# Out-projection by seven products for all eight token tiles, and norm one's scale and offset moved behind the transposes

## The chip, the cores and the metric

The kernel runs on one NeuronCore of a Trainium2 chip. The metric is the device time of one execution in microseconds. Four compute engines matter: PE (TensorE, matrix products), DVE (VectorE), ACT (ScalarE) and POOL (GpSimd). SP issues most of the transfers; in the changed kernel POOL issues some too. Each engine executes its own queue in order, and the queues meet at semaphores.

## The reference

One layer of a post-norm encoder on 1024 tokens of 1024 features, in float32. What matters here is the second half:

```python
mix = (gate_a * y_a + gate_b * y_b) @ w_out[l]
x = layer_norm(DEEPNORM_ALPHA * x + mix, ln1_g[l], ln1_b[l])
gu = x @ w_ffn_in[l]
g, u = jnp.split(gu, 2, axis=-1)
ffn = (jax.nn.silu(g) * u) @ w_ffn_out[l]
x = layer_norm(DEEPNORM_ALPHA * x + ffn, ln2_g[l], ln2_b[l])
```

`y_a` is a windowed attention, `y_b` a stick-breaking attention, and `layer_norm` takes mean and variance over the 1024 features of a token (epsilon 1e-5), then multiplies by a gain g and adds an offset b. `DEEPNORM_ALPHA` is 2 to the power 1/4; the kernel calls it ALPHA.

## The kernel before

**Precision.** Every matrix operand is split in two parts: `split` writes a rounded high part (a cast, on ACT) and the remainder (a subtraction, on DVE). A product is three matmuls: high times high, high times low, low times high. `mm3` issues them for a list of operand pairs, lines 116, 117 and 119. A matmul of 128 by 128 by 512 is written 128x512 below.

**Seven products.** A 2 by 2 block product can be formed with seven block products in place of eight, after sums of blocks on both sides (Strassen's scheme in Winograd's form). The FFN uses it for all tokens (`pair_steps`, matmuls on line 179, `run_pairs` sets the order), the down projection too (line 1512). The out-projection uses it for the first four token tiles only.

**Stages.** In-projections and gates, the two attentions with their branch projections, then: branch B's projection (`yBps`, loop over feature tiles c in the order 6, 7, 5, 4, 2, 3, 1, 0; n counts them), whose result is multiplied by the gate and added to branch A's, giving the transposed mix `mA`; `m_sums` forms its block sums as soon as two blocks exist, and `high` splits the others. Then the out-projection: for the token tiles tt 0 to 3 products p in the order 1, 2, 6, 5, 7, 3, 4 with two token tiles each (line 1369, weights' sums loaded and split by `begin_wo`, lines 550 and 551); after each, `take_in` adds the bank `ops` to the tile `acc` (x times ALPHA, line 1348). For tt 4 to 7 plain products by `mm3`, the two column halves one after the other. When a token tile has both halves, `norm_1` works on it (`layer_norm`, lines 1183 to 1191): statistics on DVE, the inverse root of the variance as a power on POOL (line 1187), then two 128x1024 operations on DVE that apply mean and g, and inverse root and b. The normed rows are stored to `x1_dr` for the residual and transposed on PE (line 1209, bank `x1ps`) by `x1_operands`, copied by ACT to `x1raw` (first four token tiles) or `x1low` (the others) and split to `x1A`.

**FFN.** `plain_half` does one column tile f = 0 by plain products, first on `x1A` of the first token half while the second half's norm ends, then on the second. Then 21 column tiles f by seven products in pairs; in each `left_f` and `right_f` load and split weights (`wlf`, `wrf`, `wbf`, `waf`, `wcf`), and `next_piece` makes one of the down projection's left operands (`left_sums`, tiles `sl`, stored to `s_dr`). Last the down products, norm two and the output.

**What sets the order.** A scheduler orders the instructions of each engine from the program's order and the dependencies; instructions marked `keep_in_program_order` stay as written. Tiles live in pools of slots by tag (`SLOTS`, 8 of tag `op`), and a new tile waits until the last reader of its slot is done. PSUM has eight banks in four tags (`BANKS`).

Of the kernel before, what the change touches and what calls it, by code (L numbers as in the profile page):

```python
# [48 lines left out]
def hybrid_trunk_kernel(ctx: ExitStack, tc, x, xt, w_first, w_v, w_in, b_gate, rel_bias, w_proj,  # L49
                        w_out, ln1_g, ln1_b, w_ffn_in, w_ffn_out, ln2_g, ln2_b, out):  # L50
# [747 lines left out]
    def value_steps(hd, g, wt):  # L798
# [9 lines left out]
        for i, kb in enumerate(kbs):  # L808
# [16 lines left out]
            def mult(i=i, kb=kb, lo_q=lo_q, n=n, pts=pts):  # L825
# [130 lines left out]
    def squash(t, c, br):  # L956
        col = br * 8 + c
        if c >= N_SQUASHED:
            tc.keep_in_program_order(
                nc.scalar.activation(t, t, AF.Sigmoid, bias=bg[:, col:col + 1]))  # L960
# [49 lines left out]

# [73 lines left out]
    m_high = [None] * 8  # L1084
    raw_22 = slot("pt", "m22")
    m_first = [slot(tag, f"m1_{kt}", F32R) for kt, tag in enumerate(("yt", "yt", "yt", "pt"))]
    m_ab = [[None] * 4 for _ in range(2)]
    acc_t = []

    def quarter(q):  # L1090
        return slice(q * 2 * P, (q + 1) * 2 * P)

    def m_sums(kt, a, b):

        put, sub = nc.vector.tensor_tensor, ALU.subtract
        g, (q0, q1, q2, q3) = m_first[kt], (quarter(q) for q in range(4))
        split(g[:, q2], g[:, q3], b[:, q0])
        nc.scalar.copy(raw_22[:, quarter(kt)], b[:, q1])
        put(b[:, q1], a[:, q1], b[:, q1], ALU.add)
        put(a[:, q1], a[:, q0], a[:, q1], sub)  # L1100
        put(a[:, q0], b[:, q1], a[:, q0], sub)
        put(b[:, q0], b[:, q0], a[:, q0], sub)
        for n, t in enumerate((a, b)):
            o = m_ab[n][kt] = slot("bw", f"m{'ab'[n]}_{kt}", F32R)
            split(o[:, LO], o[:, HI], t[:, LO])
# [533 lines left out]
```

## Time and profile before

| what | value |
|---|---|
| median of three runs | 1413.27 us (1411.41 to 1413.41) |
| profiled execution | 1412.51 us, its span 1410.7 us |
| granted TensorE clock, mean | 0.999 |
| PE busy | 1399.7 us, 99% of the span |
| DVE busy | 1034.1 us, 73% |
| ACT busy | 699.0 us, 50% |
| POOL busy | 236.0 us, 17% |
| seven products of the out-projection | 681.64 us, for 38.08 us, 168 matmuls |
| first matmul of the FFN's `plain_half` | at 766.72 us |

The span runs from the first instruction to the last. A busy share is the time in which an engine executes, over the span; PE overlaps successive matmuls, so each has a duration of 389 ns and starts about 227 ns after the one before it. In rows of a group, the columns are line, engine, operation, names written and read, shape and count, then the busy time, the mean of one in ns, and the idle time before it with what ended it. In rows of a timeline the first number is the start and the second the duration.

### The profile page before, as it was taken

The numbers are of one execution on the slowest core, as the hardware profiler recorded it, in microseconds if no ns is written. First come the engines' busy times: TensorE is split into PE (matmuls) and PEld (weight loads), VectorE is DVE, ScalarE is ACT, GpSimd is POOL, SyncE is SP. The second block draws the span as 40 slices with busy tenths as digits, with TensorE's granted clock in tenths as the row PEclk, the third lists the DMA queues.
The fourth block names the chain that finished last, engine by engine and source line by source line (L and its number), as shares of the span: only waits on it lengthen the run. The fifth ranks groups of instructions, "written<-read, shape, count | busy, mean of one in ns | idle before, by whom it ended". The sixth has DMA issues, their size and how long they took to land.

```text
span 1410.7 us, 18935 instructions
## 1 busy us (share of the span) xinstructions
PE 1399.7 (99%) x6642; PEld 1164.6 (83%) x6642; DVE 1034.1 (73%) x1671; ACT 699.0 (50%) x1245; POOL 236.0 (17%) x308
## 2 busy tenths in 40 slices
PE   9999999999999999999999999999999999999997
PEld 7888888888888888888888888888888888888886
DVE  8967657545887788878998967767677765847666
ACT  6544444545888888774413644434444443322220
POOL 0000000002555878750001000000000000000033
PEclk9999999999999999999999999999999999999999
DMA  7476468856676478755651144433444349996652
GB/s 254 165 286 224 178 236 303 295 179 238 212 231 208 130 252 281 253 198 194 231 202 75 61 148 166 149 141 143 164 164 149 143 144 342 411 385 236 233 194 90
DMA packets 98927, 292.28 MB, mean 207 GB/s; under 512 B 9728, under 2 KB 26112, under 8 KB 98832
## 3 DMA queue, kind: packets, MB, share of 16 engines
q1 hardware_dynamic: 98832, 291.07, 58.2%
q8 instruction: 52, 0.85, 0.3%
q14 instruction: 43, 0.35, 0.1%
HBM read 187.20 MB, written 100.17 MB: 204 GB/s over the span
## 4 chain that ended last, share of the span: by engine, by line
PE 94%; DVE 2%; DMA 1%; ACT 1%; issue 1%; POOL 0%; DVEq 0%; SPq 0%; ACTq 0%; POOLq 0%
PE sxf L179 16%; PE d L1512 15%; PE sxp L179 9%; PE szf L179 8%; PE v L481 5%; PE gps L606 4%; PE szp L179 4%; PE syf L179 4%; PE yAps L910 3%; PE ops L1369 3%; PE syp L179 2%; PE tp_b L817 2%; PE tp_a L817 2%; PE plain L347 1%; PE pv_b L833 1%; PE pv_b L832 1%
## 5 line engine op out<-in xcount | busy, mean ns | idle before, releaser
L1512 PE MATMUL d<-wd,sl 128*128 128x512 f32 (+1 forms) x924 | 207.7, 387 | 0.0
L1512 PEld LDWEIGHTS d<-wd,sl 128*128 128x128 f32 x924 | 172.3, 188 | 35.4
L1532 POOL TENSOR_TENSOR mv<-mv,neghalf 128x1 f32<-128x1 f32 x8 | 9.0, 1121 | 606.7 <-DVE mv L1531 606.7
L109 ACT CAST wd<-wd 128x512 fp32r<-128x512 f32 x77 | 45.9, 621 | 114.1 <-PE d L1512 66.8
L794 POOL TENSOR_TENSOR w_b<-w_b,kp_b 128x511 f32<-128x511 f32 (+3 forms) x96 | 96.0, 1012 | 23.2 <-DVE kp_b L789 16.7
L110 DVE TENSOR_TENSOR sl<-h,sl 128x512 fp32r<-128x512 f32 x77 | 52.6, 686 | 27.6 <-ACT sl L109 27.6
L789 DVE TENSOR_TENSOR_SCAN kp_b<-kp_b,ident_ps 128x512 f32<-128x512 f32 (+2 forms) x64 | 56.5, 885 | 21.0 <-ACT kp_b L786 20.0
L109 ACT CAST sl<-h 128x512 fp32r<-128x512 f32 x77 | 47.5, 620 | 48.1 <-PE syf L179 18.3
L1489 DVE TENSOR_TENSOR x<-d,x 128x512 f32<-128x512 f32 (+1 forms) x41 | 27.6, 675 | 47.6 <-PE d L1512 47.5
L786 ACT ACTIVATE kp_b<-sc_b 128x512 f32<-128x512 f32 (+3 forms) x96 | 48.3, 504 | 28.0 <-PE sc_b L706 23.6
L110 DVE TENSOR_TENSOR wd<-wd,wd 128x512 fp32r<-128x512 f32 x77 | 52.7, 709 | 10.7 <-ACT wd L109 10.6
L179 PE MATMUL szf<-x1S63h,wcf 128*128 128x512 f32 x168 | 55.1, 389 | 0.0
L110 DVE TENSOR_TENSOR pt_b<-tp_b,pt_b 128x512 fp32r<-128x512 f32 (+1 forms) x96 | 49.9, 544 | 6.6 <-ACT pt_b L109 5.7
L729 POOL MEMSET bias<- 64x64 f32 x2 | 0.3, 145 | 314.3 <-ACT bias L725 314.3
L109 ACT CAST pt_b<-tp_b 128x512 fp32r<-128x512 f32 (+1 forms) x96 | 46.6, 503 | 8.0 <-PE tp_b L817 7.6
L759 POOL TENSOR_SCALAR w_a<-w_a,st_a 128x640 f32<-128x640 f32 (+2 forms) x64 | 42.2, 669 | 48.0 <-PE sc_a L706 26.6
L754 ACT ACTIVATE w_a<-w_a,st_a 128x640 f32<-128x640 f32 (+2 forms) x64 | 44.7, 700 | 8.6 <-DVE st_a L748 7.5
L787 ACT ACTIVATE w_b<-sc_b 128x511 f32<-128x511 f32 (+3 forms) x96 | 48.3, 504 | 0.0
L817 PE MATMUL tp_b<-ident,w_b 128*128 128x128 f32 x288 | 47.3, 272 | 0.2
L110 DVE TENSOR_TENSOR pt_a<-tp_a,pt_a 128x512 fp32r<-128x512 f32 (+1 forms) x96 | 44.6, 486 | 3.3 <-ACT pt_a L109 2.2
L1307 ACT ACTIVATE h<-sxf 128x512 f32<-128x512 f32 x21 | 12.6, 598 | 68.2 <-PE sxf L179 68.2
L817 PEld LDWEIGHTS tp_b<-ident,w_b 128*128 128x128 f32 x288 | 36.4, 140 | 11.1 <-DVE pt_b L110 1.1
(1574 smaller groups left out, 4285.2 us busy)
## 6 DMA issues: line engine op xcount, KB each, us to landing
s_dr<-sl SPq DMA_DIRECT2D x77, 512.0 KB, 2.6
sl<-s_dr SPq DMA_DIRECT2D x77, 512.0 KB, 7.6
wLf<-in_w_ffn_in_dram SPq DMA_DIRECT2D x22, 512.0 KB, 4.3
wRf<-in_w_ffn_in_dram SPq DMA_DIRECT2D x22, 512.0 KB, 3.6
wd<-in_w_ffn_out_dram SPq DMA_DIRECT2D x22, 512.0 KB, 8.2
v_dr<-vc SPq DMA_DIRECT2D x16, 512.0 KB, 3.4
qs<-q_dr SPq DMA_DIRECT2D x16, 512.0 KB, 6.7
kh<-k_dr SPq DMA_DIRECT2D x16, 512.0 KB, 6.5
```

The source lines that it names most:

```text
L109: return (nc.scalar.copy(dst_h, src), nc.vector.tensor_tensor(dst_l, src, dst_h.bitcast(F32), ALU.subtract))
L110: nc.vector.tensor_tensor(dst_l, src, dst_h.bitcast(F32), ALU.subtract))
L179: mm(acc, lw[:, ks], rx, start=(first and kt == i == 0), stop=(kt == 3 and i == 2), skip_group_check=not first)
L481: mm(accs[j], a, b, start=(first and kt == n == 0), stop=(kt == 3 and n == 2), skip_group_check=True)
L606: mm(acc[hf], lw[:, ks], rx[k][:, (LO, HI)[hf]], start=(k == j == 0), stop=(k == KT - 1 and j == 2))
L754: nc.scalar.activation(s[:, 0:w], s[:, 0:w], AF.Exp, bias=st[:, m:m + 1], scale=-1.0, accum_out=st[:, 2:3])
L786: nc.scalar.activation(kp[:, c0:e], sc[:, 0:n], AF.Sigmoid, scale=-1.0)
L787: nc.scalar.activation(be[:, m0:e], sc[:, m0 - c0:n], AF.Sigmoid)
L789: nc.vector.tensor_tensor_scan(kp[:, 0:e], kp[:, 0:e], ident_ps()[:, 0:e], 0.0, ALU.mult, ALU.add)
L794: nc.gpsimd.tensor_tensor(be[:, m0:e], be[:, m0:e], kp[:, m0 - 1:e - 1], ALU.mult)
L817: ins = tr(tp[:, (qb - lo_q) * P:(qb - lo_q + 1) * P], wt[qb - q0][:, (kb - qb) * P:(kb - qb + 1) * P], ident)
L1512: mm(part, a, b, start=(fresh and i == k == 0), stop=(i == n - 1 and k == 2), skip_group_check=not fresh)
```

## The change

- The out-projection goes by seven products for all eight token tiles (`project_out(p, j)`, four token tiles j per product, p in the order 1, 2, 5, 3, 6, 7, 4). Sums and splits of the mix and of the weights are set beside its tiles and beside branch B by a table `aside`.
- Everything in this stage is divided by ALPHA: products 1, 5 and 3 are scaled by ACT into `acc`, and POOL's queue adds the rows of x by an adding DMA (`plus`); products 2, 6, 7 and 4 are added by DVE.
- The orders of DVE, ACT and POOL's queue in this stage are written out as chains (`chain`, `chain_s`, `tied`): each instruction comes after the one before it in its lane.
- `norm_1` forms only (x - mean) times the inverse root: power and one multiply on POOL, one activation of 128x1024 on ACT. g and b are applied behind the transposes, where a feature is a partition: ACT's copy out of the bank has a scale and a bias (`scaled`, from a small tile `gb_1`).
- The rows stored in `x1_dr` have neither g nor b. During the FFN POOL loads half a row tile, loads g, multiplies, stores (`scale_x1`, two pieces for each of the eight token tiles, behind the eleven of `left_sums`), and adds b by an adding DMA.
- f = 1 of the FFN has its seven right operands split ahead of time (`split_f1`); the signs of some sums change; in the down stage ALPHA is applied with each addition (`take_down`).

```diff
-    for p in (1, 2, 6, 5, 7, 3, 4):
...
-        for j in range(2):
...
-            take_in(t0 + j, cs, accs[j], scale)
-            if p in (3, 4):
-                norm_1(t0 + j)
...
-    for hf, cs in enumerate((LO, HI)):
-        for tt in range(4, 8):
...
-            mm3(acc, pairs)
-            take_in(tt, cs, acc)
...
+    def project_out(p, j):
+        accs = by if p in (2, 5, 3) else bx
+        first = p in (1, 2, 5)
+        if first:
+            accs[j] = bank(("tr", "tr", "tr", "pv")[j] if accs is by
+                           else ("mm", "mm", "sc", "sc")[j], f"ops{p}_{j}")
+        for i, kt in enumerate(KT_ORDER):
...
+            for n, (a, b) in enumerate(((lh, wh), (lh, wl), (ll, wh))):
+                mm(accs[j], a, b, start=(first and i == n == 0), stop=(i == 3 and n == 2),
+                   skip_group_check=not first)
+        tt, cs = j + 4 * (p in (5, 7, 4)), (LO, HI)[p in (5, 7, 3, 6)]
...
+        if p in (1, 5, 3):
+            chain_s(nc.scalar.activation(t, accs[j], AF.Copy, scale=1 / ALPHA))
+            plus(t, x_rows(tt, cs))
+        else:
+            chain(nc.vector.scalar_tensor_tensor(t, accs[j], 1 / ALPHA, t, ALU.mult, ALU.add))
...
+    for p in OUT[:5]:
+        for j in range(4):
+            project_out(p, j)
+            for work in aside[p, j]:
+                work()
+            if p == 6:
+                norm_1(j)
+    for n, (p, j) in enumerate(((7, 0), (7, 1), (4, 0), (7, 2), (4, 1), (7, 3), (4, 2), (4, 3))):
+        project_out(p, j)
+        if n > 3:
+            x1_operands(0, acc_t, (n - 4,))
+        if p == 4:
+            norm_1(j + 4)
...
-        nc.vector.scalar_tensor_tensor(t, t, mv[:, 0:1], g, ALU.subtract, ALU.mult)
-        if quick:
-            for cs in cuts:
-                nc.vector.scalar_tensor_tensor(t[:, cs], t[:, cs], mv[:, 2:3], b[:, cs],
-                                               ALU.mult, ALU.add)
...
+    def norm_1(tt):
+        mv, t = statistics(f"1_{tt}", 2, chain), acc_t[tt]
+        nc.gpsimd.tensor_scalar(mv[:, 3:4], mv[:, 0:1], mv[:, 2:3], -1.0, ALU.mult, ALU.mult)
+        chain_s(nc.scalar.activation(t, t, AF.Identity, bias=mv[:, 3:4], scale=mv[:, 2:3]))
...
-                    nc.scalar.copy(part, tps[i])
-                    split(o[:, LO], o[:, HI], part)
+                    scaled(part, tps[i], kt + 4 * i)
+                    halve(o[:, LO], o[:, HI], part)
...
+    def scaled(dst, src, k):
+        chain_s(nc.scalar.activation(dst, src, AF.Identity, bias=gb_1[:, 8 + k:9 + k],
+                                     scale=gb_1[:, k:k + 1]))
...
+    aside = {
...
+        (2, 0): [part(sum_4, 2), part(wo_split, 3, 1)],
+        (2, 1): [part(sum_4, 3), part(wo_split, 3, 0)],
...
+        (6, 2): [part(wo_split, 4, 1)],
+        (6, 3): [part(wo_split, 4, 0)]}
...
+    def scale_x1(tt, cs):
+
+        t, queue = slot("op", f"x1g{tt}_{cs.start}"), nc.gpsimd
+        queue.dma_start(t[:, LO], x1_dr[tt][:, cs])
+        queue.dma_start(t[:, HI], rows_of(ln1_g, cs))
+        queue.tensor_tensor(t[:, LO], t[:, LO], t[:, HI], ALU.mult)
+        queue.dma_start(x1_dr[tt][:, cs], t[:, LO])
+        done = [tt - 1] * (cs == LO and tt > 0) + [7] * (cs == HI and tt == 7)
+        for k in done:
+            queue.dma_start(x1_dr[k], rows_of(ln1_b, slice(0, D)), accum_op=ALU.add)
```

In the excerpts a row is line, operation, tile written, tiles read and shape. `ops_0`, `ops_1`, `ops_2` are the banks of token tiles j = 0, 1, 2, `m` the split mix, `woh` and `wol` the weights' high parts and remainders, `acc` the rows of a token tile; the last number tells copies of a name apart.

On PE, before, the end of product 3 and the start of product 4 in the seven products (bank `ops_0_7289`):

```order
L1369 MATMUL ops_1_7414<-wh_o_1_7432,mb_7106 128x512
L1369 MATMUL ops_1_7414<-wh_o_1_7432,mb_7153 128x512
L1369 MATMUL ops_1_7414<-wl_o_1_7433,mb_7153 128x512
L1369 MATMUL ops_1_7414<-wh_o_1_7432,mb_7153 128x512
L1369 MATMUL ops_0_7289<-wh_ot_0_7472,m22h 128x512
L1369 MATMUL ops_0_7289<-wl_ot_0_7473,m22h 128x512
```

In the changed kernel, on PE, the end of (7, tile 1) and the start of product 4 on tile 0's bank:

```order
L1411 MATMUL ops_1_7250<-wol_0_7587,m_0_7603 128x512
L1411 MATMUL ops_1_7250<-woh_0_7586,m_0_7603 128x512
L1411 MATMUL ops_2_7273<-woh_1_7565,m_2_7594 128x512
L1411 MATMUL ops_2_7273<-wol_1_7566,m_2_7594 128x512
L1411 MATMUL ops_2_7273<-woh_1_7565,m_2_7594 128x512
L1411 MATMUL ops_2_7273<-woh_1_7565,m_3_7597 128x512
L1411 MATMUL ops_0_7219<-woh_1_7658,m_2_7093 128x512
L1411 MATMUL ops_0_7219<-wol_1_7659,m_2_7093 128x512
```

Before, three tiles of other banks lay between product 7's and product 4's work on one bank; now one tile and four matmuls do, and the rest of (7, tile 2) follows behind (4, tile 0).

On DVE, before, the end of the seven products (`ln1g` and `ln1b` are g and b on all partitions):

```order
L1348 SCALAR_TENSOR_TENSOR acc_7054<-acc_7054,ops_0_7400 128x512
L1183 BN_STATS bn_0_7493<-acc_7054 128x6
L1186 BN_AGGR mv_0_7494<-bn_0_7493 128x2
L1188 SCALAR_TENSOR_TENSOR acc_7054<-acc_7054,mv_0_7494,ln1g 128x1024
L1191 SCALAR_TENSOR_TENSOR acc_7054<-acc_7054,mv_0_7494,ln1b 128x1024
L1348 SCALAR_TENSOR_TENSOR acc_7056<-acc_7056,ops_1_7414 128x512
```

In the changed kernel, on DVE, product 6's tiles 2 and 3, up to the eviction of (7, tile 0):

```order
L1419 SCALAR_TENSOR_TENSOR acc_7165<-ops_2_7273,acc_7165 128x512
L1207 BN_STATS bn_2_7558<-acc_7165 128x6
L110 TENSOR_TENSOR wol_1_7659<-wor_1_7590,woh_1_7658 128x1024
L1215 BN_AGGR mv_2_7662<-bn_2_7558 128x2
L1419 SCALAR_TENSOR_TENSOR acc_7166<-ops_3_7296,acc_7166 128x512
L1207 BN_STATS bn_3_7583<-acc_7166 128x6
L110 TENSOR_TENSOR wol_0_7682<-wor_0_7592,woh_0_7681 128x1024
L1215 BN_AGGR mv_3_7685<-bn_3_7583 128x2
L1419 SCALAR_TENSOR_TENSOR acc_7399<-ops_0_7219,acc_7399 128x512
```

The two 128x1024 operations of a norm have left DVE; the remainders of product 4's weights stand ahead of the statistics' end, and the eviction that frees the bank stands behind both.

On ACT, before, the transposed tiles of the first token half:

```order
L1219 COPY x1raw_7791<-x1ps_1_7781 128x512
L1219 COPY x1raw_7791<-x1ps_5_7786 128x512
L109 CAST x1A_1_7792<-x1raw_7791 128x512
L109 CAST x1A_1_7796<-x1raw_7791 128x512
L1219 COPY x1raw_7810<-x1ps_2_7800 128x512
```

In the changed kernel, on ACT, the last of them with the norms of token tiles 6 and 7:

```order
L109 CAST x1A_2_7866<-x1raw_7861 128x512
L1397 ACTIVATE acc_7403<-acc_7403,mv_6_7870 128x1024
L1226 ACTIVATE x1raw_7899<-x1ps_3_7889,gb_7209 128x512
L109 CAST x1A_3_7900<-x1raw_7899 128x512
L1226 ACTIVATE x1raw_7899<-x1ps_7_7894,gb_7209 128x512
L109 CAST x1A_3_7904<-x1raw_7899 128x512
L1397 ACTIVATE acc_7405<-acc_7405,mv_7_7908 128x1024
L109 CAST wf_4_7914<-wLf_7213 128x512
```

The norms, which DVE carried, now stand in ACT's queue between the copies of the transposed tiles.

More of the change, by code (lines that the diff above doesn't have):

```diff
@@ L167, in product @@
     def product(acc, W, ops, p, first):
-        if p == 3:
+        if "all" in W:
+            wh, wl = (W["all"][p][:, cs] for cs in (LO, HI))
+        elif p == 3:
             wh, wl = W["c"][:, LO], W["c"][:, HI]
@@ L1081, in hybrid_trunk_kernel, with tied, chain, chain_s @@
     fill_until(1e9)
[L1084 to L1105, printed above, removed]
+    acc_t, m_raw = [], {}
+    m_ops = {p: [None] * 4 for p in range(1, 8)}
+    wo = {}
+    OUT = (1, 2, 5, 3, 6, 7, 4)
+    KT_ORDER = (2, 3, 1, 0)
+    put, sub = nc.vector.tensor_tensor, ALU.subtract
+    lanes = dict(s=last_y[:1], v=last_y[1:])
+    def tied(lane, ins):
+        for before in lanes.get(lane, ()):
+            tc.add_manual_dep(ins.ins, before.ins.name, mybir.DependencyInfo(
+                mybir.DependencyClass.NoSync, mybir.DependencyReason.DATA), reason="lane")
+        lanes[lane] = [ins]
+        return ins
+    def chain(ins):
+        return tied("v", ins)
+    def chain_s(ins):
+        return tied("s", ins)
+    def halve(dst_h, dst_l, src):
+        hi, lo = split(dst_h, dst_l, src)
+        chain_s(hi)
+        chain(lo)
+    def plus(dst, src):
+        tied("p", nc.gpsimd.dma_start(dst, src, accum_op=ALU.add))
+    def x_rows(tt, cs):
+        return x[tt * P:(tt + 1) * P, cs]
     def more_acc(tag):
@@ new lines, in sum_3, with sum_1, sum_2, sum_4 @@
+    def sum_3(kt):
+        a = m_raw[kt + 4]
+        chain(put(a[:, LO], a[:, HI], a[:, LO], sub))
+    def sum_1(kt):
+        a, b = m_raw[kt + 4], m_raw[kt]
+        chain(put(a[:, HI], a[:, HI], b[:, HI], ALU.add))
+    def sum_2(kt):
+        a, b = m_raw[kt + 4], m_raw[kt]
+        chain(put(b[:, HI], b[:, HI], a[:, LO], ALU.add))
+    def sum_4(kt):
+        b = m_raw[kt]
+        chain(put(b[:, LO], b[:, LO], b[:, HI], sub))
+        m_split(3, kt)
+    def part(f, *args):
+        return lambda: f(*args)
@@ L1228, in x1_operands @@
                     part = low[:, (LO, HI)[i]]
-                    nc.scalar.copy(part, tps[i])
+                    scaled(part, tps[i], kt + 4 * i)
                     split(o[:, LO], o[:, HI], part)
@@ new lines, in split_f0, with split_f1 @@
+    def split_f0(n):
+        key, t, tag = (("hl", L0, "op"), ("hr", R0, "bw"))[n]
+        h, l = Wf[0][key] = [slot(tag, f"wf0{key}{i}", F32R) for i in "hl"]
+        halve(h, l, t)
+    def split_f1(p):
+        src, terms, tag = {1: (x_, (), "op"), 5: (x_, (y_, x_), "bw"), 6: (x_, (u_, x_), "bw"),
+                           2: (z_, (), "op"), 4: (z_, (z_, x_), "bw"), 7: (y_, (y_, u_), "bw"),
+                           3: (u_, (), "bw")}[p]
+        if terms:
+            chain(put(src, *terms, sub))
+        o = Wf[1].setdefault("all", {})[p] = slot(tag, f"wf1_{p}", F32R)
+        halve(o[:, LO], o[:, HI], src)
@@ new lines, in hybrid_trunk_kernel @@
+    for p in OUT[:5]:
[11 more added lines that the diff above has]
+            norm_1(j + 4)
+        if n == 1:
+            split_f1(2)
+            for tt in range(4):
+                dma(x1_dr[tt], acc_t[tt])
@@ L1422, in hybrid_trunk_kernel @@
+    for p in (4, 7, 3):
+        split_f1(p)
+    with tc.issue_after(wo["last"].ins), tc.issue_after(lanes["v"][0].ins):
+        left_f(2)
     first_h = []
```

375 lines of the change are left out of this document (167 added, 208 removed).

## The prediction

> **What bounds the kernel now.** I read the page first (busy shares, the chain of the work that ended last), then the waits of the matmul engine, then a table by stage, and last the durations around the out-projection.
>
> ```profile
> PE 1399.7 (99%) x6642; PEld 1164.6 (83%) x6642; DVE 1034.1 (73%) x1671; ACT 699.0 (50%) x1245; POOL 236.0 (17%) x308
> PE 94%; DVE 2%; DMA 1%; ACT 1%; issue 1%; POOL 0%; DVEq 0%; SPq 0%; ACTq 0%; POOLq 0%
> PE warm L266 <- DVE warm L263: 1.2, 1, 1.2
> PE gps L606 <- ACT gate L611: 0.2, 1, 0.2
> 681.64 38.08 PE ops L1369 x168
> ```
>
> PE is the bound: busy 1399.7 of 1410.7 us, 94% of the chain, and its largest wait is 1.2 us, at the start. A matmul taken away therefore saves one slot, 38.08/168 = 0.2267 us (last row, from the chain: the seven products of the four first token tiles), unless the wait that is now hidden behind it comes out. By stage (columns PE, PEld, DVE, ACT, POOL busy with their counts, granted clock, DMA share, GB/s):
>
> ```profile
> 660.00:681.50 21.50, 21.50 (x97) 17.80 (x96) 20.17 (x40) 9.40 (x19) 0.00 (x0) 1.00 0.58 198
> 681.50:720.00 38.50, 38.50 (x171) 31.90 (x170) 34.73 (x49) 16.36 (x19) 1.13 (x2) 1.00 0.74 260
> 720.00:767.00 47.00, 47.00 (x225) 39.24 (x224) 43.02 (x62) 12.94 (x21) 5.08 (x5) 1.00 0.28 101
> 767.00:781.00 14.00, 14.00 (x78) 11.62 (x77) 10.58 (x16) 8.20 (x17) 1.58 (x1) 1.00 0.20 77
> 880.00:918.00 38.00, 38.00 (x170) 31.45 (x169) 27.03 (x37) 16.55 (x25) 0.00 (x0) 1.00 0.41 152
> ```
>
> From 660 to 767 (end of branch B, out-projection) DVE is busy 90 to 94%: the second engine is nearly full just where the change works. In the FFN (880 to 918) it has 29% to spare and POOL does nothing.
>
> **The change part by part.** Rows for the terms:
>
> ```profile
> L1348 DVE SCALAR_TENSOR_TENSOR acc<-acc,ops 128x512 f32<-128x512 f32 x22 | 14.6, 681 | 4.4 <-PE ops L1369 3.3 <-PE ops L119 1.1
> L1183 DVE BATCH_NORM_STATS2 bn<-acc 128x6 f32<-128x512 f32 x16 | 10.7, 687 | 0.3
> L1188 DVE SCALAR_TENSOR_TENSOR acc<-acc,mv,ln1g 128x1024 f32<-128x1024 f32 x8 | 10.4, 1296 | 0.2
> L551 DVE TENSOR_TENSOR wl_ot<-wr_ot,wh_ot 128x1024 fp32r<-128x1024 f32 x8 | 9.5, 1218 | 0.0
> L110 DVE TENSOR_TENSOR x1A<-x1raw,x1A 128x512 fp32r<-128x512 f32 x8 | 5.3, 682 | 0.0
> L550 ACT CAST wh_ot<-wr_ot 128x1024 fp32r<-128x1024 f32 x7 | 7.4, 1054 | 10.3 <-PE ops L1369 5.7 <-DMA wr_ot<-wt_drt 3.3 <-DVE ma L110 1.1
> L109 ACT CAST mb<-mA 128x512 fp32r<-128x512 f32 x2 | 1.2, 620 | 0.8 <-DVE mA L1102 0.8
> L1219 ACT COPY x1raw<-x1ps 128x512 f32<-128x512 f32 x8 | 4.3, 594 | 6.2 <-PE x1ps L1209 6.1
> L960 ACT ACTIVATE gB<-gB,bg x4: 1150/1150/1152, 641.9 to 657.2; 128x1024 f32<-128x1024 f32 x4
> L1187 POOL TENSOR_TENSOR mv<-mv,neghalf x8: 547/694/1583, 713.5 to 768.7; 128x1 f32<-128x1 f32 x8
> L90 POOL MEMSET neghalf<- x1: 98/98/98, 0.9 to 0.9; 128x1 f32 x1
> ```
>
> *Matmuls.* The out-projection had 168 + 192 of 128x512 and has 7 products x 4 tiles x 4 x 3 = 336: 24 x 0.2267 = **-5.44 us**. The clock is 1.00 in every row above, so no gain waits there.
>
> *Branch B (n = 5, 6).* Sums and splits of the out-projection's operands now stand here. One projection of 24 matmuls is 5.44 us on PE; the DVE work placed beside it sums to 5.57: a lag under 1 us, which two banks a half absorb. Cost 0; were the cover gone, 4 x 0.13.
>
> *Product 2.* Behind tiles 0 and 1 the two lanes alternate: eviction 0.68 and sum_4 0.68 on DVE, cast 0.62 on ACT, its remainder 0.68 on DVE, the weight's cast 1.05 beside that, its remainder 1.22: 0.68 + 0.68 + 0.62 + 1.05 + 1.22 and handoffs (DVE to DVE 0.03, 766.92 to 767.65 below) = 4.3, less what is started early, say 4.1 against 2.72 of PE (12 slots). DVE is then 3.3 us late (0.5 of it older). Products 5 and 3 bring DVE 21.7 us of work in 21.8, so the lag stays. The evictions of 1, 5 and 3 have gone to ACT, x arriving by an adding DMA: nobody needs that sum for 10 us.
>
> *Stall 1, product 4 on product 7's bank.* Count time from the start of the out-projection on PE, 2.72 a tile: the five first products end at 54.4. In product 6 DVE's order puts the remainders of product 4's weights ahead of the statistics of tiles 2 and 3, and those ahead of the eviction of (7, tile 0); ACT's puts each norm ahead of a cast that DVE waits for. From the eviction of (6, 0) at 49.6: + 0.68 + 0.69 + 0.21 + POOL 1.1 -> norm 0 at 52.2, norm 1 53.7 to 54.9, cast 55.9, remainder 57.1, statistics and POOL 1.3, norm 2 58.4 to 59.5, cast 60.5, remainder 61.7, statistics, eviction of (7, 0) until 62.45. (POOL 1.1: the power 0.55, a 128x1 multiply between the rows 0.10 and 0.55, taken 0.27, the rest handoffs.) PE comes back to that bank at 54.4 + 2 x 2.72 + 4 x 0.227 = 60.75. **+1.7 us**; between 0 (no lag from product 2) and 3 (the 4.3 without overlap, twice, and the POOL link at 1.6).
>
> *Stall 2, the last norm.* What stood there before, with its slack (the last row, from the chain, gives a transpose as 1.77/16 = 0.11):
>
> ```profile
> 766.72 0.39 PE L116 MATMUL plainhl_0f<-x1A,wlf0h 128*128 128x512 f32 x1
> 766.92 0.69 DVE L1348 SCALAR_TENSOR_TENSOR acc<-acc,ops 128x512 f32<-128x512 f32 x1 [0.73 <-PE ops L119]
> 767.65 0.69 DVE L1183 BATCH_NORM_STATS2 bn<-acc 128x6 f32<-128x512 f32 x1
> 768.37 0.21 DVE L1186 BATCH_NORM_AGGREGATE mv<-bn 128x2 f32<-128x12 f32 x1
> 768.62 1.28 DVE L1188 SCALAR_TENSOR_TENSOR acc<-acc,mv,ln1g 128x1024 f32<-128x1024 f32 x1
> 768.73 1.58 POOL L1187 TENSOR_TENSOR mv<-mv,neghalf 128x1 f32<-128x1 f32 x1 [3.86 <-DVE mv L1186]
> 770.34 1.28 DVE L1191 SCALAR_TENSOR_TENSOR acc<-acc,mv,ln1b 128x1024 f32<-128x1024 f32 x1 [0.44 <-POOL mv L1187]
> 772.17 1.61 PE L1209 MATMUL x1ps<-ident,acc 128*128 128x128 f32 x13
> 747.82 1.77 PE x1ps L1209 x16
> ```
>
> From the last slot of the out-projection to the transposes 5.45 us, exactly 24 matmuls: no stall, and no slack either. Now ACT carries casts, the scaled copies and all norms in one fixed order. From the end of (4, 1), E: four ACT operations for the first transposed tile (two of 0.59, two of 0.62) end at E + 3.0, the remainder 0.68, statistics 0.21, POOL 1.1 -> norm 5 from 5.1 to 6.25; tiles two and three of the transposes 10.95; remainder, statistics, POOL -> norm 6 13.0 to 14.15; fourth tile 16.6, remainder 17.3, statistics, POOL, slowed by a two-input DVE subtraction that starts beside it (+0.43) -> norm 7 18.8 to 19.95. PE would be at these transposes at E + 3 x 2.72 + 32 x 0.11 + 24 x 0.2267 = 17.1. So **+2.8 us**, part of it (0.8) already as a wait for the fourth tile's remainder; between 1 (PE arrives later by stall 1's remainder, the norms start sooner) and 5 (each of three POOL links 1.0 longer).
>
> *FFN start.* The next transposes' banks are read by ACT behind four casts of f 1 and f 2: **+0.4**, from 0 to 1.
>
> *FFN.* GpSimd now scales the stored rows: per tile two loads of 256 KB, two of a row of g, two multiplies, two stores and an adding DMA. Its queue held nothing here. DVE's two-input operations may be held by 16 multiplies of about 1.0 (first row): 16 us over 380, against 11 us idle in each 38. Cost 0, unless the slots come back late.
>
> ```profile
> L794 POOL TENSOR_TENSOR w_b<-w_b,kp_b 128x511 f32<-128x511 f32 (+3 forms) x96 | 96.0, 1012 | 23.2 <-DVE kp_b L789 16.7
> s_dr<-sl SPq DMA_DIRECT2D x77, 512.0 KB, 2.6
> sl<-s_dr SPq DMA_DIRECT2D x77, 512.0 KB, 7.6
> 941.52 0.62 ACT L109 CAST wcf<-wRf 128x512 fp32r<-128x512 f32 x1 [1.70 <-DMA s_dr<-sl]
> 945.64 0.60 ACT L1307 ACTIVATE h<-sxf 128x512 f32<-128x512 f32 x1 [1.66 <-PE sxf L179]
> 948.36 0.59 ACT L198 COPY gt<-sxf 128x512 f32<-128x512 f32 x1 [2.12 <-PE sxf L179]
> 950.85 0.62 ACT L109 CAST sl<-h 128x512 fp32r<-128x512 f32 x1 [1.90 <-PE syf L179]
> ```
>
> No DMA of GpSimd's queue moves bulk data in the trace. By its nearest rows a transfer is between 2.6 and 7.6 us: load, multiply, store take 6.2 to 16.2. The second slot is free to load about 13.2 us after the cast at 941.52 (a piece like the one at 950.85, and its store) and is wanted, one period of 19.04 later, by a cast that must start by +26.1 for the copy at 948.36 + 19.04 to be in time for PE: 12.9 us of room. I take the lower end, since these are 256 KB beside a DMA share of 0.41, and keep the upper. [...]
>
> *Rest.* The down stage's 128x512 additions (L1489, mean 675 ns) become 681 ns ones; SP has seven issues less, and one load more at the start, far ahead of its use: 0.
>
> **Sum:** -5.44 + 1.7 + 2.8 + 0.4 = -0.54 us against the profiled 1412.51, which is 0.76 below the median; against the median 1413.27 - 0.54 = **1412.7 us**. About 0.2% (2.8 us) is what a measurement of this kernel can tell from no change.
>
> **Rivals.** *A: no stalls, the whole gain.* For it: DVE's work from branch B to the first FFN half falls from 160 to 140 us as I add up the instructions of the new order, and a lag that vanishes in products 5 and 3 removes stall 1. Against: the last chain is on ACT, which only gets more work. 1413.3 - 5.4 + 0.4 = **1408.2**.
>
> *B: GpSimd's transfers hold the slots, slower.* Place: ACT's queue at the cast that reuses a scaling slot; behind it wait a copy of 0.59 and with it PE. It decides from 12.9 us, that is when each transfer is over 5.9 us. At 6.5 each, 14.0 - 12.9 = 1.1 us in each of eight pairs: 1412.7 + 8.8 = **1421.5**; at 7.6, 26 more. For it only the row of 7.6; against it the row of 2.6 and an empty queue.
>
> *C: the power waits for DVE each time.* Its row has 547 ns at best and 1583 when an operation with two SBUF inputs had just started on DVE (768.62, power at 768.73, over 0.4 after that operation's end). If norms 5, 6 and 7 all meet it, 3 x 1.03 more: **1415.8**, within no change or just past it. [...]
>
> **How the numbers follow.** The ledger's case (-3 to +2.3, the three stalls between 2.4 and 7.7 together) 0.45; A 0.30; C and longer lanes 0.13, half of it past 2.8 us; B 0.12. Faster: A, 0.30, and some 0.02 of the ledger's edge. Slower: B 0.12 and 0.06. Same: 0.50. The range goes from A less a little, 1407.8, to 1418: above C, with B's worse half outside.
>
> **What would show it.** After: PE 24 matmuls of 128x512 fewer; a PE wait on DVE of 1.7 where it comes to (4, 0), about 60.8 us into the out-projection; one on ACT before the transposes of the last token tile of 2 to 3, after a short wait on DVE; PE without waits in the FFN. Wrong, if the first wait is missing (DVE was not late: A), if the FFN's period is over 19.04 us (B), or if the powers of norms 5 to 7 are all 1.5 us (C).

## The result, and the profile after

The changed kernel takes 1444.65 us (median of 4 runs, 1441.1 to 1445.99) against 1412.57 us (1411.41 to 1413.41; four runs, the three of the table above and one more): a ratio of 1.0224, 95% interval 1.0203 to 1.0244. It is 32 us slower, outside the range of the prediction; the profiled execution is 1445.99 us, its span 1444.2.

The page after, its first and fourth parts (busy shares; the chain that ended last by engine and by line, which is followed back only to 857 us, so that its shares sum to 39%):

```profile
PE 1407.0 (97%) x6618; PEld 1164.2 (81%) x6618; DVE 1021.5 (71%) x1653; ACT 716.2 (50%) x1265; POOL 298.5 (21%) x400
PE 26%; DMA 6%; DVE 3%; ACT 2%; issue 1%; POOL 1%; DVEq 0%; ACTq 0%; POOLq 0%
PE d L1578 14%; PE sxf L182 7%; DMA s_dr<-sl 3%; PE szf L182 3%; DMA x1g<-in_ln_g_dram 2%; PE syf L182 2%; DMA x_dr<-x1g 2%; ACT sl L109 1%; DVE sl L110 1%; POOL x1g L1382 1%; DVE h L1340 0%; POOL x1g L1380 0%; ACT wcf L109 0%; ACT gt L1334 0%; DVE wcf L110 0%
```

PE has its 24 matmuls less (6618 for 6642), and the chain, as far back as it goes, is no longer nearly all PE: `x1g`, the scaling tile of the FFN, and `s_dr`, the stores of `sl`, stand in it. What PE waited for in the FFN, the out-projection and the transition between them (total, times, longest):

```profile
PE sxf L182 <- ACT h L210: 11.9, 7, 3.6
PE sxf L182 <- ACT gt L201: 7.7, 6, 1.8
PE sxf L182 <- DVE gt L197: 2.2, 1, 2.2
PE ops L1411 <- DVE acc L1419: 1.8, 1, 1.8
PE x1ps L1236 <- ACT acc L1397: 1.6, 1, 1.6
PE plainhl_0f L116 <- ACT x1A L109: 0.5, 1, 0.5
PE plainhl_0f L117 <- DVE x1A L110: 0.4, 2, 0.2
```

The last four rows are the out-projection and the transition, 4.3 us; the first three are the FFN, where before had none. By stage the same is seen in PE's busy time and in the granted clock (columns as before):

```profile
681.50:720.00 38.50, 38.50 (x172) 31.87 (x171) 31.20 (x44) 20.67 (x32) 8.05 (x9) 1.00 0.69 180
720.00:767.00 47.00, 45.18 (x216) 37.48 (x215) 34.28 (x61) 25.84 (x34) 8.32 (x17) 1.00 0.47 145
767.00:781.00 14.00, 11.42 (x58) 8.24 (x57) 7.35 (x13) 10.37 (x17) 1.08 (x2) 1.00 0.18 75
850.00:900.00 50.00, 44.64 (x188) 35.81 (x187) 27.68 (x38) 16.83 (x26) 11.04 (x14) 0.97 0.55 186
950.00:1000.00 50.00, 45.49 (x186) 37.00 (x187) 31.19 (x43) 18.76 (x29) 6.83 (x9) 0.93 0.56 192
```

I took the starts of the groups of matmuls from the two traces. From the first matmul of the out-projection to the first `szf` group (third product of f = 1) it is 124.9 us before (681.48 to 806.34) and 124.9 after (681.89 to 806.75): the stage neither wins nor loses. From there to the first matmul of the down stage it is 386.7 us before (806.34 to 1193.04) and 419.6 after (806.75 to 1226.30): 32.9 us, all of the loss. Of these, 24.2 are 14 gaps, counted from the start of one matmul to the start of the next, less 0.227. (The profile counts idle time from the end of a matmul, 0.16 us less for each gap: 21.9.) The rest is mostly matmuls at a lower clock behind some of the gaps (last section).

One pair of the FFN in the changed kernel, rows of POOL, then of ACT, then of PE (others between them are left out):

```profile
889.54 0.58 POOL L1380 DMA_DIRECT2D x1g<-x_dr  x1 [27.61 <-DMA s_dr<-sl]
890.72 0.55 POOL L1380 DMA_DIRECT2D x1g<-x_dr  x1
894.27 1.29 POOL L1382 TENSOR_TENSOR x1g<-x1g 128x512 f32<-128x512 f32 x1 [2.46 <-DMA x1g<-in_ln_g_dram]
895.97 0.57 POOL L1383 DMA_DIRECT2D x_dr<-x1g  x1 [0.41 <-POOL x1g L1382]
```

```profile
872.25 0.62 ACT L109 CAST wcf<-wRf 128x512 fp32r<-128x512 f32 x1 [0.62 <-DMA s_dr<-sl]
893.99 0.62 ACT L109 CAST sl<-h 128x512 fp32r<-128x512 f32 x1 [4.85 <-PE szf L182]
899.69 0.62 ACT L109 CAST wcf<-wRf 128x512 fp32r<-128x512 f32 x1 [5.08 <-DMA x_dr<-x1g]
903.19 0.58 ACT L201 COPY gt<-sxf 128x512 f32<-128x512 f32 x1
```

```profile
903.82 0.50 PE L182 MATMUL sxf<-x1S56h,wbf6h 128*128 128x512 f32 x1 [1.71 <-ACT gt L201]
```

The scaling tile waits for a slot until a store of `sl` has landed (889.54), loads, multiplies and stores until 899.46, and the cast of `wcf` waits 5.08 us for that slot. Behind it in ACT's queue, after three more operations, stands the copy of 903.19, which frees the bank of PE's next product; PE waits 1.71 us for it. That is the place which rival B named.

### The profile page after: what moved, and what is told of

It is laid out like the page before. It is cut to its first block, busy times and chain, and to the rows that moved or that the text cites. A ratio compares the mean times of both kernels' runs of the same rounds, so it can differ in the third digit from the quotient of the medians.

```text
span 1444.2 us, 19099 instructions
## 1 busy us (share of the span) xinstructions
PE 1407.0 (97%) x6618; PEld 1164.2 (81%) x6618; DVE 1021.5 (71%) x1653; ACT 716.2 (50%) x1265; POOL 298.5 (21%) x400
## 5 line engine op out<-in xcount | busy, mean ns | idle before, releaser
L1554 DVE SCALAR_TENSOR_TENSOR x<-d,x 128x512 f32<-128x512 f32 (+1 forms) x57 | 38.6, 679 | 59.5 <-PE d L1578 59.5
L1216 POOL TENSOR_TENSOR mv<-mv,neghalf 128x1 f32<-128x1 f32 x16 | 12.6, 785 | 293.8 <-DVE mv L1215 293.8
L1411 PE MATMUL ops<-woh,m 128*128 128x512 f32 x224 | 70.2, 391 | 1.8 <-DVE acc L1419 1.8
L1380 POOL DMA_DIRECT2D x1g<-x_dr x16 | 9.0, 564 | 285.6 <-DMA s_dr<-sl 193.5
L182 PE MATMUL szf<-x1S73h,wcf 128*128 128x512 f32 x160 | 52.5, 389 | 0.0
L1411 PEld LDWEIGHTS ops<-woh,m 128*128 128x128 f32 x224 | 42.0, 188 | 10.9 <-issue 2.2
```

The costliest lines, as they stand in the source:

```text
L182: mm(acc, lw[:, ks], rx, start=(first and kt == i == 0), stop=(kt == 3 and i == 2), skip_group_check=not first)
L1411: mm(accs[j], a, b, start=(first and i == n == 0), stop=(i == 3 and n == 2), skip_group_check=not first)
```

## The experiments

My theory was the slots: ACT's casts wait for slots that the scaling tiles hold. The rivals were the transfers themselves (they slow the stores of `sl`) and what I call the port: GpSimd's multiplies and DVE's two-input operations hold each other up (in the changed kernel a remainder of `sl` took 1.47 us beside a multiply, at 894.64, against 0.69 at 935.89 with none beside it; the multiply of 936.75 took 1.58 beside DVE's product of 936.50, against 1.29 for the median of the sixteen). In the diffs, `+` and `-` are against the kernel named; every ratio is against runs of the kernel before.

**Without the scaling; in another pool; its transfers alone; without its multiply.** Against the changed kernel.

```diff
e1_no_scale:
-                ] + ([lambda: scale_x1(q, LO), lambda: scale_x1(q, HI)] if q < 8 else [])
+                ]
e2_kp:
-        t, queue = slot("op", f"x1g{tt}_{cs.start}"), nc.gpsimd
+        t, queue = slot("kp", f"x1g{tt}_{cs.start}"), nc.gpsimd
e5_traffic:
-        t, queue = slot("op", f"x1g{tt}_{cs.start}"), nc.gpsimd
+        t, queue = dram(f"x1s{tt}_{cs.start}_", 1)[0], nc.gpsimd
-        queue.tensor_tensor(t[:, LO], t[:, LO], t[:, HI], ALU.mult)
e3_no_mult:
-        queue.tensor_tensor(t[:, LO], t[:, LO], t[:, HI], ALU.mult)
```

> The changed kernel without the scaling of the stored rows during the FFN (no GpSimd work there; the residual lacks g and b, which this run leaves out). The FFN of the changed kernel is 32.9 us longer than before's (806.7 to 1226.1 against 806.3 to 1192.8), 24.2 of it gaps between matmuls. Every theory that blames this work expects the loss gone: 1444.7 - 33 = 1411 to 1412 us, the out-projection's net with its stalls of 1.8 and 1.6. If 1420 or more remains, something else of the change (seven operand splits of f 1, signs of sums) costs time in the FFN.

Measured: 1412.5 us, ratio 1.0000 (0.9991 to 1.0009). The loss is gone, and the rest of the change is worth nothing measurable.

> The scaling tiles take slots of tag kp instead of op; transfers, multiplies and sums are the same. Slots (my theory: ACT's cast of wcf waits for a slot that a scaling tile holds until its store has landed, 10 us, and the copies for PE stand behind it): no wait of wcf on a scaling store; kp has one slot to spare, so most of the 33 us goes, 1412 to 1422. Traffic (the adding transfers and the extra loads slow the stores of sl, which free the slots) or port (DVE and GpSimd exclude each other): 1440 to 1446 as the changed kernel.

Measured: 1415.63 us, ratio 1.0033 (1.0019 to 1.0047), the FFN 388.9 us against 386.7 in e1. With the same transfers and multiplies, 29 of the 32 us are gone. So neither transfers nor the port cost the loss as such. But the transfers are not free, as the issues between 845 and 1000 us show (name, queue, count, size, median us to landing), of e2:

```profile
s_dr<-sl SPq DMA_DIRECT2D x29, 512.0 KB, 4.3
x1g<-x_dr POOLq DMA_DIRECT2D x8, 256.0 KB, 3.5
x1g<-in_ln_g_dram POOLq DMA_DIRECT2D x8, 256.0 KB, 5.1
x_dr<-x1g POOLq DMA_DIRECT2D x8, 256.0 KB, 2.4
x_dr<-in_ln_b_dram POOLq DMA_DIRECT2D x4, 512.0 KB, 7.6
```

and of before, in the same stretch:

```profile
s_dr<-sl SPq DMA_DIRECT2D x29, 512.0 KB, 2.6
```

In the changed kernel, in the same stretch:

```profile
s_dr<-sl SPq DMA_DIRECT2D x25, 512.0 KB, 2.9
x1g<-x_dr POOLq DMA_DIRECT2D x8, 256.0 KB, 3.9
x1g<-in_ln_g_dram POOLq DMA_DIRECT2D x8, 256.0 KB, 4.1
x_dr<-x1g POOLq DMA_DIRECT2D x8, 256.0 KB, 2.7
```

In e2 a store of `sl` lands 1.7 us later beside them than before; ACT has room for that, and PE lost 1.3 us in waits.

> GpSimd's queue issues the same transfers with the same sizes, but through a scratch buffer in HBM, not a slot, and without the multiply (left out: the scaling by g). Slots: 1411 to 1413, no waits in the FFN. Traffic: most of the 33 us stays, over 1435; a third of it, over 1420, would already say that transfers count. Port: 1411 to 1413 too.

Measured: 1451.49 us, ratio 1.0281 (1.0266 to 1.0297), but not for the reason it was built for. With no slot to wait for, the transfers of the rows went out right behind the stores of the normed rows, around the transition (DMA share 0.85 between 780 and 800 us), and the last norms' powers stood behind them in POOL's queue: PE waited 8.9 us for `x1raw` and 5.3 for a norm; the FFN itself took 386.7 us, as in e1. Also the stages ahead of the out-projection came out 19 us longer. Its trace points to the sixteen loads of g: they no longer wait for a slot either, and were issued between 1.3 and 20.7 us, beside the first loads of the kernel's inputs. PE waited 6.8 us for `xh` there and had a granted clock of 0.91 in the first 100 us, against 1.00 in the changed kernel. The run says nothing on transfers spread over the FFN.

> The scaling tiles stay in op slots with all their transfers, the multiply on GpSimd alone is left out (rows are stored unscaled). Port: the loss goes, 1412. Slots: each slot is held some 1.7 us less of 10, in eight pairs, so 8 to 14 us less: 1430 to 1437. Traffic: within 3 us of the changed kernel, 1442 to 1447.

Measured: 1430.87 us, ratio 1.0131 (1.0116 to 1.0146): what the slots expected, not what the port did.

**Is it the place of the pieces, the number of slots, the length of the turn?** The first and the last three against the changed kernel, the two with a held slot against e1.

```diff
e6_spread (order of the 13 pieces; the two of the scaling were the last):
+        [out(1), out(4), put, scale_x1(q, LO), put, out(5), put, out(2), out(7), put, scale_x1(q, HI), out(6), out(3)]
e10_hold, e14_hold (a tile of op from f = 3; its last reader):
+            held.append(slot("op", "held"))
e10:  +      nc.gpsimd.tensor_tensor(held_out, held[0][:, 0:8], held[0][:, 0:8], ALU.mult)
e14:  +      nc.gpsimd.tensor_tensor(held_out, held[0][:, 0:8], Wf[i + 1]["L"][:, 0:8], ALU.mult)
e15_no_store:
-        queue.dma_start(x1_dr[tt][:, cs], t[:, LO])
e16_sp_op (the other load and the store in the same way):
-        queue.dma_start(t[:, LO], x1_dr[tt][:, cs])
+        dma(t[:, LO], x1_dr[tt][:, cs])
e18_own:
-        t, queue = slot("op", f"x1g{tt}_{cs.start}"), nc.gpsimd
+        if not own:
+            own.append(slot("op", "x1g"))
+        t, queue = own[0], nc.gpsimd
```

> The changed kernel with the two scaling pieces of a pair set apart: one behind the third of the eleven other pieces, one behind the ninth, both still in op slots. Slots: in the changed kernel both tiles take their slots within 1.2 us of each other (loads at 889.54 and 890.72), late, and the next cast of wcf wants one of them at once; apart, each has another follower, and the loss of 33 us should fall by half or more: 1420 to 1430. If it is only the number of slots (15 tiles where 13 were, in 38 us), it stays: 1438 to 1448.

Measured: 1449.78 us, ratio 1.0268 (1.0255 to 1.0281). Missed: setting them apart, so that other casts take the slots, does not help; it costs 5 us more.

> No scaling at all (left out, as in e1, which runs in 1412.5), but one of the eight op slots is held by an idle tile from the fourth to about the seventeenth column tile of the FFN: no transfer, no multiply. Slots: casts wait for stores of sl, PE for the copies behind them, as in the changed kernel: at least 10 us more than e1, 1423 to 1445, and the waits end when the tile is given back. Traffic or port: no change, 1412 to 1413.

Measured: 1412.75 us, ratio 1.0003 (0.9994 to 1.0012). Inconclusive: the read that should give the slot back ran at 805.4 us, 0.2 us after the write, so nothing was held. It was repeated with a read that cannot come early:

> No scaling (left out). One op slot is held by an idle tile from the FFN's start until the weights of column tile 18 have landed, some 300 us, by a read that waits for that load (in e10 the read came at 805.4, at once, so nothing was held). Number of slots: at least 10 us more than e1, 1423 or more. Turn of a slot (what costs is that one slot's turn lasts two transfers, a load and a store, just ahead of a cast in ACT's queue): seven slots that turn fast still do, 1412 to 1416.

Measured: 1414.05 us, ratio 1.0010 (1.0001 to 1.0019). The slot was held for 267 us:

```profile
L1501 POOL MEMSET held<- x1: 105/105/105, 804.7 to 804.7; 128x8 f32 x1
L1505 POOL TENSOR_TENSOR held_out<-held,wLf x1: 203/203/203, 1071.9 to 1071.9; 128x8 f32<-128x8 f32 x1
```

In this execution the FFN took 386.5 us, against 386.7 in e1, and PE waited for nothing in it; 1.4 us more than in e1 stand as a wait in the in-projections. Seven slots do as well as eight: it is not the number.

> The changed kernel, tiles in op, loads and multiply kept, the store of the scaled rows left out: a tile is free 3.5 to 4 us sooner (issue 0.57, landing 2.6 to 3.6). e3 took 1.7 us out of each turn and won 13.8 us, 8 us for each. Turn of a slot: 1444.7 - 8 x 3.5 = 1417, at most back to 1412.5. If the loads' late start alone counts: within 5 us of the changed kernel.

Measured: 1442.08 us, ratio 1.0214 (1.0185 to 1.0243). Missed: taking 3.5 us out of the turn won 2.6 in all, and the intervals of the two kernels overlap. ACT's waits for scaling tiles and for stores of `sl` in the FFN show why, first of e15, then of the changed kernel:

```profile
ACT sl L109 <- POOL x1g L1382: 46.1, 8, 7.0
ACT wcf L109 <- DMA s_dr<-sl: 11.8, 8, 2.4
ACT sl L109 <- DMA s_dr<-sl: 6.4, 6, 1.8
```

```profile
ACT wcf L109 <- DMA x_dr<-x1g: 26.7, 6, 5.2
ACT sl L109 <- DMA s_dr<-sl: 24.0, 12, 4.0
ACT sl L109 <- DMA x_dr<-x1g: 6.6, 2, 4.9
ACT wcf L109 <- DMA s_dr<-sl: 8.2, 9, 2.2
```

With the store gone, the slot is handed to another cast: not to `wcf`, but to `sl`, which stands earlier in ACT's queue, and which now waits for the multiply. I read this as the earlier follower taking back what the shorter turn wins.

> The changed kernel, tiles in op, the scaling's loads and stores on SP's queue. Turn of a slot: a turn is shorter by four issues of 0.56 and by 1 us for a load, 2 to 3 us: 1444.7 - 8 x 2.5 = 1425. Rival (the queue is what counts, software descriptors as such): nearly all goes, 1412 to 1416. Rival (SP's queue, held by a store that waits, delays the stores of sl): 1445 or more.

Measured: 1433.82 us, ratio 1.0142 (1.0125 to 1.0160). Part of the loss goes, between two expectations; `wcf` still waits for the scaling's store (15.0 us in seven waits).

> The changed kernel, all transfers, multiplies and sums as they are on GpSimd's queue, but all sixteen pieces use one and the same tile, which keeps one of the eight op slots for itself; seven turn for the casts. No cast of ACT can then wait for a scaling piece. Who takes the slot next (the casts of wcf or sl stand directly behind the scaling in a slot's turn, and ACT's queue behind them): the loss goes but for e14's 1.6: 1414 to 1415. Number of slots together with traffic: 1420 or more.

Measured: 1477.93 us, ratio 1.0456 (1.0439 to 1.0474). Missed, and by much. With one tile the pieces were no longer spaced by slots: all sixteen ran one after the other from 846 to 1001 us. What ACT waited for between 760 and 1260 us:

```profile
ACT sl L109 <- DMA x_dr<-x1g: 49.1, 1, 49.1
ACT sl L109 <- DMA s_dr<-sl: 30.5, 14, 6.7
ACT wcf L109 <- DMA s_dr<-sl: 22.9, 12, 4.9
```

The 49.1 us are a single wait: a later `sl` was given this slot, and its cast stood until the sixteenth piece was stored. This is the suspected mechanism in its plainest form, but by my own construction. The second row speaks for the rival: while the transfers run without a pause, stores of `sl` land so late that casts wait up to 6.7 us for them though none waits for a scaling tile. Up to that long wait PE had lost some 15 us so. So the transfers do count where they are dense; in e2, spread over the FFN, they cost 2.2.

**The out-projection's two stalls, and a better version.** e7 to e9 are against e2, the others against the kernel named.

```diff
e7_stats6, e8_stats (statistics and GpSimd's part as stat_1, the activation stays in norm_1):
             project_out(p, j)
+            if p == 6:
+                stat_1(j)
             for work in aside[p, j]:
...
e8 only:
         project_out(p, j)
+        if p == 4:
+            stat_1(j + 4)
         if n > 3:
             x1_operands(0, acc_t, (n - 4,))
e9_kp_spread: e8 with the order of e6
e11_kp_no_mult: e8 without queue.tensor_tensor(...)
e12_stats_noscale: e8 without scale_x1
e13_sp: e8 with the transfers of e16, and
-    for p in (4, 7, 3):
-        split_f1(p)
...
     plain_half(LO, ops_1[1] + ops_1[2], second_half)
+    for p in (4, 7, 3):
+        split_f1(p)
e17_best: e13 with m_split(3, kt) behind wo_split(3, ...) instead of inside sum_4
-        (2, 0): [part(sum_4, 2), part(wo_split, 3, 1)],
+        (2, 0): [part(sum_4, 2), part(wo_split, 3, 1), part(m_split, 3, 2)],
...
e19_best_own: e17 with the one tile of e18
```

> Scaling tiles in kp, and in product 6 the statistics of a tile (DVE, GpSimd) ahead of product 4's weight splits, the norm itself where it was. The prediction's stall 1: the wait of PE on DVE at (4, 0), 1.8 us in the changed kernel, falls to under 0.3, since the eviction of (7, 0) then comes some 2.4 us earlier: 1415.6 - 1.8 = 1413.8. Rival (DVE late from product 2 alone): the wait stays over 1.2, 1415 to 1416.

Measured: 1415.1 us, ratio 1.0020 (1.0011 to 1.0029). The wait at (4, 0) falls from 1.8 to 0.7. The time falls by 0.5, which the two intervals do not tell from nothing; the profiled execution has a wait of 2.0 in the FFN, and e2's had none so long.

> As the one before, and for token tiles 4 to 7 too the statistics go ahead of the remainders of the transposed tiles on DVE. The prediction's stall 2: the waits before the last transposes (1.7 on ACT, 0.5 and 0.4 for the transposed tiles) go, since norm 7 then starts at E + 14 instead of E + 18.8: 1413.8 - 2.6 = 1411.2, with the slowed matmuls behind that gap 0.5 to 1 less. Rival (ACT is full there): the order on DVE changes nothing, 1413 to 1414.

Measured: 1412.59 us, ratio 1.0000 (0.9991 to 1.0008). The 1.7 before the last transposes and the 0.5 and 0.4 are gone, and a wait of 1.2 on `x1low` stands in their place. The stage is 121.3 us against 124.9.

> As e8, with the two scaling pieces set apart as in e6. The 2.2 us that are still lost in the FFN with the tiles in kp (1194.40 against 1192.22 without the scaling, where the last product of the FFN's up stage ends) go if each of the two meets a free slot: 1411.2 - 2.2 = 1409.0. If they are GpSimd's multiplies holding up DVE, they stay: 1411.

Measured: 1412.8 us, ratio 1.0002 (0.9993 to 1.0011). No gain from setting the pieces apart here either.

> As e8 (1412.6, tiles in kp), with GpSimd's multiply left out. The FFN of e8 is 2.5 us longer than without scaling. Port: that goes, 1410. Slots: it goes only in part, 1411 to 1412.5, since the tiles still wait for three transfers.

Measured: 1410.51 us, ratio 0.9993 (0.9981 to 1.0004), runs from 1408.28 to 1415.62: too wide to tell the two expectations apart.

> As e8 with no scaling of the stored rows (left out): what the change of the out-projection alone would bring with its statistics early. e8's stage is 3.6 us shorter than the changed kernel's (121.28 against 124.85 from the first matmul of the out-projection to the first product of f 1's third step), and the FFN is that of e1: 1412.5 - 3.6 = 1408.9, 0.25% under before. If it is 1411 or more, the stage's gain is given back later.

Measured: 1409.26 us, ratio 0.9975 (0.9965 to 0.9986). As expected: this is what the out-projection can bring once its stalls are short.

> As e8, the scaling's loads and stores on SP's queue in place of GpSimd's, and three splits of f 1's operands behind the last transposes. Slots: a kp tile is held shorter (2.6 us a transfer against 3.6 to 3.9 and 0.56 of issue each), the FFN's loss falls from 2.5 to under 1; the wait of 1.2 of the last transposes on x1low goes: 1412.6 - 2.7 = 1409.9. Rival (a store that waits for the multiply holds up the stores of sl behind it on SP): the FFN gets longer, 1413 to 1420.

Measured: 1409.89 us, ratio 0.9982 (0.9974 to 0.9991), with the whole computation. In kp the transfers on SP's queue do no harm. Two things were changed at once, and the traces tell them apart: the wait on `x1low` is gone and the stage is 120.4 us against 121.3, the FFN 387.5 against 389.1.

> As e13, and in product 2 the weight's cast and remainder are put between sum_4 and the split of its result, so that DVE does not wait for ACT twice per tile (about 0.8 us less in each of two tiles). The prediction's lag: the wait at (4, 0), 0.7 in e13, goes: 1409.9 - 0.9 = 1409.0. If the lag comes from elsewhere the wait stays, 1409.9.

Measured: 1409.26 us, ratio 0.9975 (0.9963 to 0.9986), the best with the whole computation, though its interval and e13's overlap. But the step that was its reason did not happen; its waits of PE, the two longest:

```profile
PE warm L269 <- DVE warm L266: 1.2, 1, 1.2
PE ops L1417 <- DVE acc L1425: 0.7, 1, 0.7
```

The 0.7 stays, so this part of the lag is not product 2's; where it comes from is open.

> As e17 (1409.3, transfers on SP's queue, two kp tiles a pair), with the one tile of its own in op instead. If who takes the slot next is all that counts, the same or up to 1 us better, 1408.3 to 1410; if SP's queue with one tile (each load waits for the store before it) holds up the stores of sl, 1412 or more.

Measured: 1441.73 us, ratio 1.0206 (1.0190 to 1.0221): as in e18 the pieces crowd together, and casts of `sl` wait up to 10.1 us for stores.

## Why the prediction was wrong

**The matmuls** held: 24 fewer.

**Stall 1** held. (Its chain, added up again with the 0.21 of the statistics' end that stands ahead of the eviction, ends at 62.6 and not at 62.45, which makes the forecast 1.9.) PE came to (4, 0) at 742.41 + 0.23, 60.75 us after 681.89, as forecast, and waited:

```profile
742.18 0.61 PE L1411 MATMUL ops<-woh,m 128*128 128x512 f32 x2
744.62 0.47 PE L1411 MATMUL ops<-woh,m 128*128 128x512 f32 x1 [1.82 <-DVE acc L1419]
```

That is 1.8 for 1.7 forecast. e7 confirms the larger part of the cause: with the statistics ahead of the weight's remainders 1.1 of it go.

**Stall 2** held within 0.3: 1.6 + 0.5 + 0.4 = 2.5 for 2.8. With E = 751.96 the norms of tiles 5, 6 and 7 start at E + 5.3, 13.8 and 19.9 (5.1, 13.0, 18.8 forecast), the last:

```profile
765.80 1.24 ACT L1397 ACTIVATE acc<-acc,mv 128x1024 f32<-128x1024 f32 x1 [1.94 <-POOL mv L1396]
766.95 0.76 ACT L1226 ACTIVATE x1raw<-x1ps,gb 128x512 f32<-128x512 f32 x1
771.90 1.24 ACT L1397 ACTIVATE acc<-acc,mv 128x1024 f32<-128x1024 f32 x1 [2.20 <-POOL mv L1396]
```

A copy with scale and bias takes 0.76 to 0.78, not the 0.59 of the plain copy that I priced it by, and the norm 1.24, not 1.15; with that and PE's own waits, both the norms and PE came later than forecast, so the small difference is in part luck. **Rival C** fell: the powers of norms 5 and 6 took 0.55 each, and that of norm 7, on POOL's timeline:

```profile
770.69 0.81 POOL L1216 TENSOR_TENSOR mv<-mv,neghalf 128x1 f32<-128x1 f32 x1 [4.92 <-DVE mv L1215]
```

**FFN start**, 0.4: no such wait is seen in the changed kernel; it came up, with 1.2, only when stall 2 was gone (e8).

So the part ahead of the FFN was forecast at -0.5 us and measured at 0.0 (e1 against before, within 0.09%). The measured terms give -5.4 + 1.8 + 2.5 = -1.1 in idle time; from start to start the five gaps cost 0.8 more, which makes -0.3. **Rival A** fell: it needed DVE's lag to vanish, and the lag was there.

**The FFN** is where the prediction failed, and the step is this sentence of it: "The second slot is free to load about 13.2 us after the cast at 941.52 [...] 12.9 us of room", on which it put the term at 0. The turn itself was inside my bounds of 6.2 to 16.2, though not at the lower end that I took: from 889.54 to 899.69, 10.15 us. The room was not 12.9. The loads began 17.3 and 18.5 us after the cast of `wcf` at 872.25. Of the 4.1 us by which the first came late, 1.7 are the store of `sl` that frees its slot: I priced it by the median of 2.6, and it took 4.3. This could have been read before: the store of the piece at 950.85 is issued at 952.47, behind two loads of weights, and takes 4.3 us there too, so the slot is free 15.3 us after the cast and not 13.2. Another 1.3 are PE, which began its `syf` group, for which this `sl` waits, 7.9 us after the cast against 6.6 before; 0.7 lie between the landing and the load's issue.

And I looked at the second tile, while the first one's slot goes to `wcf`. By the prediction's own deadline, 26.1 us after the cast, that leaves 8.8 us of room for a turn of 10.15: the cast of `wcf` came 27.4 us after the one before it, 1.3 late, and PE waited 1.7. In seven of the eight pairs a cast waits 3.4 to 5.2 us for a scaling tile, in the remaining pair two casts wait 2.6 and 1.7. The order of the changed kernel could have shown who takes each slot; I counted slots and trusted a mean slack. Rival B had the place and the sign, and a chance of only 0.12. Its condition, transfers of over 5.9 us, did not come true (medians of 2.7 to 4.1 above), because it and its price (8.8, or 26 at the worst) hung on the same room.

e1 and e2 show that the scaling tiles in this pool cost 29 of the 32 us, and e3, with the multiply gone, fits a price for the time in which they hold a slot. e14 shows that it is not how many slots there are, and e15 that a shorter turn helps little when an earlier cast takes the slot. That the price is set by which cast takes the slot next I read from ACT's waits in the changed kernel, e15 and e18; no run shows it alone, and e6, which changed the followers, was slower.

How the 32.9 us divide between the direct wait and the slower stores of `sl` is not settled. I took, ahead of each of the 14 gaps, ACT's last wait of over 0.7 us for a scaling tile or a store of `sl`. Eleven gaps, 13.5 us of idle time, follow a cast that waited for a scaling tile. Three, of 2.25, 3.58 and 2.62 us, follow a cast of `sl` that waited for a store of `sl`, the middle one this:

```profile
951.51 0.62 ACT L109 CAST sl<-h 128x512 fp32r<-128x512 f32 x1 [2.12 <-DMA s_dr<-sl]
```

These three stores took 6.4, 8.8 and 7.9 us. Some in e2 took up to 7.8, and PE waited 1.3 us there in all; I read this as a late store costing much only where the scaling tiles hold slots of the same pool too. Of a slot of kp the followers are different ones, and one of the four is spare; that this is why kp does it is argued, not shown.

## What to carry to other kernels

Work on an idle engine is not hidden if its buffers turn in a pool that a busy engine's in-order queue draws from (29 of the 32 us here, by e2): for each new tile, look up which instruction takes its slot next, when it wants it, and when the very transfer lands that frees the slot, rather than counting free slots, taking a median or comparing busy shares. A load, an operation and a store in one turn of a slot are 10 us here, where a cast, its remainder and a store are about 4 (0.62 + 0.69 + 2.6). And removing work from the bound engine bought nothing until the two waits that it uncovered were taken out by moving the statistics forward: that, and the other pool with SP's queue, brought the time 0.25% under before's.

## What the runs showed that I had not expected

Behind some gaps PE ran at about half speed. In the changed kernel, behind a wait of 3.58 us:

```profile
952.67 0.79 PE L182 MATMUL sxf<-x1S73h,waf8h 128*128 128x512 f32 x1 [3.58 <-ACT h L210]
953.26 0.63 PE L182 MATMUL sxf<-x1S73l,waf8h 128*128 128x512 f32 x1
953.69 0.63 PE L182 MATMUL sxf<-x1S73h,waf8l 128*128 128x512 f32 x1
```

The matmuls start 0.43 us apart for some 3 us, then 0.227 again; by windows the granted clock is 0.76 from 950 to 957 us and 1.00 in the 7 us behind. In this FFN it followed the three longest of the 14 gaps (2.25, 2.62 and 3.58 us of idle time) and one of 1.85, for 1.6 to 1.8 us of loss each, and not one of 1.88 nor the shorter ones. So a stall of PE can cost more than its own length. The length alone does not tell when: in the FFNs of all the runs the six gaps from 3.10 us up were followed by slow matmuls, but of the 34 between 1.8 and 3.1 us only 16 were. In e15 gaps of 2.95 and 2.97 were, 2.83 and 2.87 were not; in e3 one of 2.57 was and one of 2.93 was not. What decides it is open.
